# A trunk layer whose last matrix product is a seven-product block scheme: its stages in another order, other PSUM banks, tiles aligned to 512 bytes, scaled sums in place

## The chip, the cores and the metric

The kernel runs on one core of a Trainium2 chip, in one launch. Its time is the device time of that launch in microseconds (us). Three runs gave 753.96, 755.59 and 756.29 us; the median is 755.59 us. Engines are named as the profile names them: PE is TensorE (PEld its weight loads), DVE is VectorE, ACT is ScalarE, POOL is GpSimd, SP issues nearly all DMAs.

## The reference, cut to what matters

One decoder layer on x (512 tokens by 1024 channels, float32). The change touches the last part only, the dense MLP and what follows it:

```python
x = x + rms_norm(merged @ w_out[l], g_mix_post[l])
h = rms_norm(x, g_ff_pre[l])
ff = jnp.square(jax.nn.relu(h @ w_ff_in[l])) @ w_ff_out[l]     # 1024 -> 4096 -> 1024
x = x + rms_norm(ff, g_ff_post[l])
```

## The kernel before, in words

Every float32 operand of a matmul is split in a high part and a low part (`whi` and `wlo`, `ah` and `al`): ACT casts to get the high part, DVE subtracts to get the low part, and each product is three matmuls (`mm3`: high times high, high times low, low times high). All weights stream through one line of chunks of 512 KB in the order of the list `plan`: SP loads a chunk into one of three `raw` buffers, ACT and DVE split it into one of six pairs `whi`, `wlo`, and a raw buffer is loaded again as soon as DVE has made the low part from it. So a chunk that is six later waits until PE is done with the pair, and a load that is three later waits for DVE.

The MLP runs in four blocks b = 0 to 3 of 1024 hidden channels (`NB`, line 938 on). In each, eight tiles f of the first product (192 matmuls in all, called here the f1 stage, sums `accf` in two PSUM banks in turn) give the hidden activations; per tile ACT takes the relu out of PSUM (`rl`) and squares it (`ec`). Two tiles make a pair m: after the second, ACT and DVE make three split operands (`ah`, `al`, 128x768), DVE forms four sums of quarters (`ec`, 128x256), and ACT and DVE split those (`ah`, `al`, 128x1024). The second product is then done in 2x2 blocks with seven products instead of eight, in four stages over the four pairs: s1 (A11 and AQ, into banks `accx` and `accz`), s2 (A12, into `accy`), s3 (AN on into `accx`, A22 into a new `accy`), s4 (AR on into `accz`, AS on into `accx`). Between the stages `gather` adds a bank into the running sums `ys` in SBUF (ACT copies in block 0 where a sum is new, DVE adds otherwise). s1, s3 and s4 use sums of weight blocks that DVE makes in `block_sums` (`t`, `raw<-raw`), s2 plain ones.

Numbering of a block's chunks: 0 to 7 belong to f1 (0 and 1 to tiles 0 and 1, 2 and 3 to tiles 2 and 3, and so on), then come 8 to 11 for s1, 12 and 13 for s2, 14 to 17 for s3, 18 to 21 for s4.

Block 0 starts before the kernel's first PSUM pool is closed: its tiles 0 to 3 (`psf`) are done in halves of 256 columns in the banks of that pool, and the second PSUM pool opens after them. A PSUM pool hands out its banks in the order in which its names first appear. The first pool has `av` in bank 0, `tr` in 1 and 2, `z` in 3 and 4, `mm` in 5 to 7; `psf` 0 to 2 lie in 5 to 7, and `psf` 3 in bank 0. In the second pool before, `accf` has banks 0 and 1, `accx` 2 and 3, `accz` 4 and 5, `accy` 6 and 7. Until the second pool opens, ACT and DVE run in the order of the program (`act.on`, `dve.on`); from then on a scheduler in the compiler orders each engine's queue.

At the end, `scaled_out` takes the sum of squares of a finished sum on ACT (`junk`, with an accumulator) and multiplies it by the gain on DVE (`yg`); `finish_out` makes the root on POOL (`pr`), does the last scale and residual add on DVE, and stores. `junk` and `yg` share one ring of four buffers (`tmp`). The last tile's bank (`accz`, token tile 3) is filled in two halves of 256 columns, and the second half's matmuls wait for the first half's gather.

Of the kernel before, what the change touches and what calls it, by code (L numbers as in the profile page):

```python
# [9 lines left out]
F32 = mybir.dt.float32  # L10
# [4 lines left out]
ALU = mybir.AluOpType  # L15
PSUM = bass.MemoryType.PSUM

P = 128
T = 512
D = 1024  # L20
NT = T // P
# [27 lines left out]
def trunk_layer(ctx: ExitStack, tc: tile.TileContext, x, w_in, w_pool, pool_scale, gm_gain,  # L49
                w_spatial, b_spatial, w_br_sb, w_br_pool, w_br_gm, w_out, g_mix_pre,  # L50
                g_mix_post, g_ff_pre, g_ff_post, w_ff_in, w_ff_out, out):
    nc = tc.nc
    x2 = x[0]
    o2 = out[0]

    cst = ctx.enter_context(tc.tile_pool(name="cst", bufs=1))
    wp = ctx.enter_context(tc.tile_pool(name="wp", bufs=1))
    sm = ctx.enter_context(tc.tile_pool(name="sm", bufs=4))
    ht = ctx.enter_context(tc.tile_pool(name="ht", bufs=1))
    dram = ctx.enter_context(tc.tile_pool(name="dram", bufs=1, space=bass.MemoryType.DRAM))  # L60

# [7 lines left out]
    def slot(ring, name, dt=F32):  # L69
        return home[0].tile([P, T], dt, name=name, tag=ring, bufs=RINGS[ring])  # L70
# [81 lines left out]
    for b in range(NB):  # L152
        for f in range(0, FT, 2):
            use["f1", b, f] = plan_cols(ff_in_k, (b * FT + f) * P)


        for stage in ("s1", "s2", "s3", "s4"):
            use[stage, b] = range(len(plan), len(plan) + (2 if stage == "s2" else FT // 2))
            for m in range(0, FT // 2, 2 if stage == "s2" else 1):
                b11, b12, b21, b22 = (  # L160
                    ff_out_k[:, b * FT + 2 * m + o:b * FT + 2 * m + o + 1, c:c + 512]
                    for o in range(2) for c in (0, 512))
                if stage == "s2":
                    plan.append([ff_out_k[:, b * FT + 2 * m + 1:b * FT + 2 * m + 4:2, :512]])
                else:
                    plan.append({"s1": [b11, b12], "s3": [b22, b21], "s4": [b12, b22]}[stage])
                    derive[len(plan) - 1] = (stage, m)
# [95 lines left out]
    def cut(pair, s):  # L263
        return pair[0][:, s], pair[1][:, s]
# [97 lines left out]
    if True:  # L362
# [31 lines left out]
        two, rs, hns, pts = {}, {}, {}, {}  # L394
        for step in V_ORDER.split():
            what = step.rstrip("0123")
            t, g = ([int(c) for c in step[len(what):]] + [0, 0])[:2]
# [218 lines left out]
        pool = [None] * 2  # L616
# [259 lines left out]
    A11, A22, A12, AQ, AN, AS, AR = range(7)  # L876
# [25 lines left out]
    ys = [[None, None] for _ in range(NT)]  # L902
    yg = [[None, None] for _ in range(NT)]
    x1b = [None] * NT

    def product(ps, part, p, m, weights, new=True, c=WHOLE):

        left = tuple(x[:, part, p * P:(p + 1) * P] for x in parts[m])
        mm3(ps[:, c], left, cut(weights, c), new and m == 0, new and m == M - 1, not new)

    def block(which, p):
        return psum.tile([P, T], F32, name="acc" + which, tag=which, bufs=2)

    def gather(t, hf, ps, op, b, c=WHOLE):

        if ys[t][hf] is None:
            ys[t][hf] = ff.tile([P, T], F32, name="ys", tag="ys", bufs=8)
            act.activation(ys[t][hf], ps, AF.Copy, scale=1.0 if op == ALU.add else -1.0)
        else:
            dve.tensor_tensor(ys[t][hf][:, c], ys[t][hf][:, c], ps[:, c], op)  # L920

    def scaled_out(t, hf, c=WHOLE):
        n = hf + (c.start > 0)
        square_sum(ys[t][hf][:, c], twos[t][:, n:n + 1])
        if c.start == 0:
            yg[t][hf] = slot("tmp", "yg")
        dve.tensor_mul(yg[t][hf][:, c], ys[t][hf][:, c], gfpost[hf][:, c])

    def finish_out(t):
# [8 lines left out]
    M = FT // 2  # L938
    for b in range(NB):
        first = 0  # L940
        if b == 0:

            first = 4
            halves = slice(0, T // 2), slice(T // 2, T)
            wks = [Weights(("f1", b, f), ahead=2 - f) for f in (0, 2)]
            pss = [bank4("mm", f, "psf") for f in range(first)]
            for f in range(first):
                ff_in(pss[f], wks[f // 2], f % 2, halves[0])
                if f in (1, 2):
                    turn(f + 1)  # L950
            early.close()
            ff = ctx.enter_context(tc.tile_pool(name="ff", bufs=1, reuse_waits="tile"))
            home[0] = ff
            RINGS["tmp"] = 4
            gfpost = bcast_row(g_ff_post[0], [ff.tile([P, T], F32, name=f"gfpost{g}")
                                              for g in range(2)])
            for f in range(first):
                if f == 1:
                    Weights(("f1", b, first))[0]
                ff_in(pss[f], wks[f // 2], f % 2, halves[1])  # L960
                ff_act(f, pss[f])
            act.on = dve.on = False
            banks.close()
            psum = ctx.enter_context(tc.tile_pool(name="psum2", bufs=1, space=PSUM,
                                                  reuse_waits="tile"))
        for f in range(first, FT):
            if f % 2 == 0:
                wk = Weights(("f1", b, f))
            ps = block("f", f)
            ff_in(ps, wk, f % 2, slice(0, T))  # L970
            ff_act(f, ps)
        final = b == NB - 1
        if final:
            for i in range(2):
                pair = ff.tile([P, 2, D], F32, name="x1b", tag="ec", bufs=2)
                for t in (2 * i, 2 * i + 1):
                    x1b[t] = pair[:, t - 2 * i, :]
                    sp.dma_start(x1b[t], x1d[t])

        def stage(name, n, keep=False):  # L980

            wk = Weights((name, b), keep=keep)
            wk.tiles = [(i, j, k) for i in use[name, b] for j in range(len(plan[i]))
                        for k in range(plan[i][j].shape[1])]
            return lambda m, j: tile_of(wk, m * n + j)

        def tile_of(wk, i):
            i, j, k = wk.tiles[i]
            wk.ready(i)
            h, l = made[i][j]  # L990
            return h[:, k, :], l[:, k, :]

        two = range(2)
        x, z = ([block(w, p) for p in two] for w in "xz")
        w = stage("s1", 2)
        for m in range(M):
            for j, ps, part in (0, x, A11), (1, z, AQ):
                for p in two:
                    product(ps[p], part, p, m, w(m, j))
        for p in two:  # L1000
            gather(2 + p, 0, x[p], ALU.add, b)
            gather(p, 1, z[p], ALU.add, b)
        y = [block("y", p) for p in two]
        w = stage("s2", 1)
        for m in range(M):
            for p in two:
                product(y[p], A12, p, m, w(m, 0))
        for p in two:
            gather(2 + p, 0, y[p], ALU.add, b)
        if final:  # L1010
            for p in two:
                scaled_out(2 + p, 0)
        y = [block("y", p) for p in two]
        w = stage("s3", 2)
        for m in range(M):
            for j, ps, part in (0, x, AN), (1, y, A22):
                for p in two:
                    product(ps[p], part, p, m, w(m, j), j == 1)
        for p in two:
            gather(2 + p, 1, x[p], ALU.subtract, b)  # L1020
            gather(p, 0, y[p], ALU.add, b)
        w = stage("s4", 2, final)
        if not final:
            for m in range(M):
                for j, ps, part in (1, z, AR), (0, x, AS):
                    for p in two:
                        product(ps[p], part, p, m, w(m, j), False)
            for p in two:
                gather(2 + p, 1, z[p], ALU.add, b)
                gather(p, 1, x[p], ALU.subtract, b)  # L1030
                gather(p, 0, x[p], ALU.add, b)
            continue
        for m in range(M):
            product(z[0], AR, 0, m, w(m, 1), False)
        gather(2, 1, z[0], ALU.add, b)
        scaled_out(2, 1)
        for p in two:
            for m in range(M):
                product(x[p], AS, p, m, w(m, 0), False)
            gather(p, 1, x[p], ALU.subtract, b)  # L1040
            gather(p, 0, x[p], ALU.add, b)
            scaled_out(p, 1)
            scaled_out(p, 0)
            if p == 0:
                finish_out(2)
            finish_out(p)
        for c in HALVES:
            for m in range(M):
                product(z[1], AR, 1, m, w(m, 1), False, c)
            gather(3, 1, z[1], ALU.add, b, c)  # L1050
            scaled_out(3, 1, c)
        finish_out(3)
# [29 lines left out]
```

## Time and profile before

| what | value |
|---|---|
| median of three runs | 755.59 us |
| the profiled execution's own time | 756.68 us |
| its span, first to last instruction | 754.8 us |
| PE busy | 716.1 us (95%), 3320 matmuls |
| DVE, ACT, POOL busy | 494.7, 353.5, 53.8 us |
| HBM traffic | 89.2 MB, mean 118 GB/s over the span |

The profile is one execution. The span leaves out some 1.9 us of the run's own time. The MLP's blocks begin on PE at about 384 us (block 0, in halves), 481.0, 566.4 and 651.8 us; the last matmul ends at about 739.8 us. Times inside the span are counted from its start.

### The profile page before, as it was taken

To read this page: it belongs to the slowest core of one execution; us is meant where nothing else is said; L and a number is where in the kernel's file an instruction comes from. 1 tells how busy PE (TensorE), PEld (TensorE's weight loads), DVE (VectorE), ACT (ScalarE), POOL (GpSimd) and SP (SyncE) were. 2 spreads that over 40 slices of the span, in tenths; PEclk is the share of its full clock that TensorE was granted. 3 is DMA by queue.
4 is the path that set the end of the run, shared out by engine and by line. 5 is a ranking of instruction groups with operands and counts; after the bars stand their busy time and mean duration, and the time that the engine had idled before them with its cause. 6 is when DMAs were issued, how large, how long until landed. Compare 5 with 4: busy or idle time off the path is not lost.

```text
span 754.8 us, 9132 instructions
## 1 busy us (share of the span) xinstructions
PE 716.1 (95%) x3320; PEld 579.5 (77%) x3320; DVE 494.7 (66%) x755; ACT 353.5 (47%) x577; POOL 53.8 (7%) x103
## 2 busy tenths in 40 slices
PE   8999999999999999999993999999999999999891
PEld 5889887787878888888883777888788877888681
DVE  6646799786866443443756575566976678665974
ACT  6566756565453332233435465355334553355431
POOL 4001112212120000000310000000000000000000
PEclk9999999999999999999997899999999999999997
DMA  8363222312224333531345136532563335533612
GB/s 278 99 185 90 78 78 60 88 56 84 85 68 127 86 110 109 189 94 52 122 133 167 56 112 178 158 111 84 163 194 117 106 116 170 167 112 116 211 63 84
DMA packets 72431, 89.80 MB, mean 119 GB/s; under 512 B 4545, under 2 KB 49729, under 8 KB 72386
## 3 DMA queue, kind: packets, MB, share of 16 engines
q1 hardware_dynamic: 72384, 89.21, 37.9%
q8 instruction: 26, 0.43, 0.2%
q14 instruction: 19, 0.16, 0.1%
q10 hardware_dynamic: 2, 0.00, 0.0%
HBM read 85.01 MB, written 4.19 MB: 118 GB/s over the span
## 4 chain that ended last, share of the span: by engine, by line
PE 81%; DVE 8%; DMA 7%; ACT 2%; issue 1%; POOL 0%; SPq 0%; DVEq 0%; POOLq 0%; ACTq 0%
PE psc L82 26%; PE accf L82 19%; PE psb L82 6%; PE acc L82 5%; PE accy L82 5%; PE accx L82 5%; DMA raw<-in_w_ff_out_dram 4%; PE accz L82 3%; PE psv L82 3%; DVE wlo L82 2%; PE psgv L82 2%; PE z L82 1%; PE pt L82 1%; DVE raw L82 1%; PE av L82 1%
## 5 line engine op out<-in xcount | busy, mean ns | idle before, releaser
L82 DVE TENSOR_TENSOR wlo<-raw,whi 128x1024 fp32r<-128x1024 f32 (+1 forms) x145 | 166.7, 1154 | 124.5 <-ACT whi L82 124.0
L82 ACT CAST whi<-raw 128x1024 fp32r<-128x1024 f32 (+1 forms) x152 | 146.6, 972 | 163.6 <-PE accf L82 37.4
L82 PE MATMUL psc<-hT,whi 128*128 128x512 f32 x576 | 184.3, 401 | 0.0
L82 PE MATMUL accf<-hT,whi 128*128 128x512 f32 x448 | 142.4, 399 | 11.9 <-ACT rl L82 11.9
L82 PEld LDWEIGHTS psc<-hT,whi 128*128 128x128 f32 x576 | 104.0, 189 | 22.7 <-issue 1.5
L82 PE MATMUL psc<-hT,wlo 128*128 128x512 f32 x288 | 113.7, 395 | 0.0
L82 PEld LDWEIGHTS accf<-hT,whi 128*128 128x128 f32 x448 | 85.3, 191 | 32.5 <-ACT rl L82 12.1
L82 PE MATMUL accf<-hT,wlo 128*128 128x512 f32 x224 | 89.3, 399 | 0.0
L82 PEld LDWEIGHTS psc<-hT,wlo 128*128 128x128 f32 x288 | 54.2, 188 | 12.8
L82 PEld LDWEIGHTS accf<-hT,wlo 128*128 128x128 f32 x224 | 42.7, 191 | 10.3
L82 ACT CAST ah<-ec 128x768 fp32r<-128x768 f32 (+1 forms) x32 | 30.2, 943 | 32.6 <-DVE ec L82 32.1
L82 DVE TENSOR_TENSOR al<-ec,ah 128x768 fp32r<-128x768 f32 (+1 forms) x32 | 34.8, 1088 | 9.6 <-ACT ah L82 9.6
L275 POOL TENSOR_TENSOR pr<-pv,mhalf 128x1 f32<-128x1 f32 x8 | 4.8, 605 | 502.7 <-DVE pv L82 502.7
L82 PE MATMUL accx<-whi,al 128*128 128x512 f32 x96 | 37.9, 395 | 0.0
L82 PE MATMUL accx<-wlo,ah 128*128 128x512 f32 x96 | 37.9, 395 | 0.0
L82 PE MATMUL accx<-whi,ah 128*128 128x512 f32 x96 | 37.9, 395 | 0.0
L82 DVE TENSOR_TENSOR ec<-ec 128x256 f32<-128x256 f32 x64 | 26.7, 422 | 14.4 <-ACT ec L82 14.1
L82 DVE TENSOR_TENSOR_SCAN nb<-nb,zeros 128x128 f32<-128x128 f32 (+3 forms) x32 | 27.5, 864 | 7.5 <-POOL nb L473 7.0
L82 PE MATMUL accz<-whi,al 128*128 128x512 f32 (+1 forms) x68 | 26.3, 387 | 5.0 <-DVE al L82 5.0
L82 PE MATMUL accz<-whi,ah 128*128 128x512 f32 (+1 forms) x68 | 26.0, 383 | 1.3 <-DVE ys L82 1.3
L82 DVE TENSOR_TENSOR raw<-raw 128x512 f32<-128x512 f32 x32 | 22.0, 687 | 6.3 <-DMA raw<-in_w_ff_out_dram 6.3
L82 ACT CAST a<-pt 128x128 fp32r<-128x128 f32 (+3 forms) x32 | 13.6, 426 | 26.4 <-PE pt L82 26.4
(186 smaller groups left out, 1204.4 us busy)
## 6 DMA issues: line engine op xcount, KB each, us to landing
raw<-in_w_ff_out_dram SPq DMA_DIRECT2D x96, 256.0 KB, 3.0
raw<-in_w_in_dram SPq DMA_DIRECT2D x42, 512.0 KB, 3.9
raw<-in_w_ff_in_dram SPq DMA_DIRECT2D x32, 512.0 KB, 4.0
xt<-in_x_dram SPq DMA_DIRECT2D x16, 256.0 KB, 6.5
raw<-in_w_out_dram SPq DMA_DIRECT2D x8, 512.0 KB, 4.1
raw<-in_w_ff_out_dram SPq DMA_DIRECT2D x8, 512.0 KB, 3.6
raw<-in_w_br_sb_dram SPq DMA_DIRECT2D x4, 512.0 KB, 3.7
x1d<-xt SPq DMA_DIRECT2D x8, 256.0 KB, 2.9
```

Source lines behind the costliest of these rows:

```text
L82: i = op(*args, **kw).ins
L275: nc.gpsimd.tensor_tensor(r, v, mhalf, ALU.pow)
```

## The change

- The stages run s2, s1, s3, s4 instead of s1, s2, s3, s4, in the list of loads too: chunks 8 and 9 of a block are now s2's, 10 to 13 s1's.
- `accz` of block 0 is allocated as soon as the second PSUM pool opens, before the first `accf`, and `accy` before `accx`. So `accz` has banks 0 and 1, `accf` 2 and 3, `accy` 4 and 5, `accx` 6 and 7.
- During the four half-width tiles, the split ahead of tile 4 goes one chunk ahead and not three.
- In s3 each pair does `accy` first and then `accx`, but for the last pair. The gathers out of `accx` come before those out of `accz`.
- In the last block the scaled sums are written in place over `ys`, but for token tile 3.
- Three unused tiles of 384, 96 and 128 bytes a partition, each set to zero by POOL at the start, push the pools behind them. Before, `raw`, `whi`, `wlo` and all large tiles started 32 bytes past a multiple of 64; now they start on a multiple of 512.

```diff
--- before.py
+++ after.py
@@ -53,9 +53,17 @@
     x2 = x[0]
     o2 = out[0]
 
+
+    def spacer(name, n):
+        pool = ctx.enter_context(tc.tile_pool(name=name, bufs=1))
+        nc.gpsimd.memset(pool.tile([P, n], F32, name=name), 0.0)
+
+    spacer("space0", 96)
     cst = ctx.enter_context(tc.tile_pool(name="cst", bufs=1))
+    spacer("space1", 24)
     wp = ctx.enter_context(tc.tile_pool(name="wp", bufs=1))
     sm = ctx.enter_context(tc.tile_pool(name="sm", bufs=4))
+    spacer("space2", 32)
     ht = ctx.enter_context(tc.tile_pool(name="ht", bufs=1))
     dram = ctx.enter_context(tc.tile_pool(name="dram", bufs=1, space=bass.MemoryType.DRAM))
 
@@ -154,7 +162,7 @@
             use["f1", b, f] = plan_cols(ff_in_k, (b * FT + f) * P)
 
 
-        for stage in ("s1", "s2", "s3", "s4"):
+        for stage in ("s2", "s1", "s3", "s4"):
             use[stage, b] = range(len(plan), len(plan) + (2 if stage == "s2" else FT // 2))
             for m in range(0, FT // 2, 2 if stage == "s2" else 1):
                 b11, b12, b21, b22 = (
@@ -923,7 +931,7 @@
         n = hf + (c.start > 0)
         square_sum(ys[t][hf][:, c], twos[t][:, n:n + 1])
         if c.start == 0:
-            yg[t][hf] = slot("tmp", "yg")
+            yg[t][hf] = slot("tmp", "yg") if t == NT - 1 else ys[t][hf]
         dve.tensor_mul(yg[t][hf][:, c], ys[t][hf][:, c], gfpost[hf][:, c])
 
     def finish_out(t):
@@ -956,13 +964,14 @@
                                               for g in range(2)])
             for f in range(first):
                 if f == 1:
-                    Weights(("f1", b, first))[0]
+                    Weights(("f1", b, first), ahead=1)[0]
                 ff_in(pss[f], wks[f // 2], f % 2, halves[1])
                 ff_act(f, pss[f])
             act.on = dve.on = False
             banks.close()
             psum = ctx.enter_context(tc.tile_pool(name="psum2", bufs=1, space=PSUM,
                                                   reuse_waits="tile"))
+            z = [block("z", p) for p in range(2)]
         for f in range(first, FT):
             if f % 2 == 0:
                 wk = Weights(("f1", b, f))
@@ -991,7 +1000,16 @@
             return h[:, k, :], l[:, k, :]
 
         two = range(2)
-        x, z = ([block(w, p) for p in two] for w in "xz")
+        y = [block("y", p) for p in two]
+        w = stage("s2", 1)
+        for m in range(M):
+            for p in two:
+                product(y[p], A12, p, m, w(m, 0))
+        for p in two:
+            gather(2 + p, 0, y[p], ALU.add, b)
+        x = [block("x", p) for p in two]
+        if b:
+            z = [block("z", p) for p in two]
         w = stage("s1", 2)
         for m in range(M):
             for j, ps, part in (0, x, A11), (1, z, AQ):
@@ -999,25 +1017,21 @@
                     product(ps[p], part, p, m, w(m, j))
         for p in two:
             gather(2 + p, 0, x[p], ALU.add, b)
-            gather(p, 1, z[p], ALU.add, b)
-        y = [block("y", p) for p in two]
-        w = stage("s2", 1)
-        for m in range(M):
-            for p in two:
-                product(y[p], A12, p, m, w(m, 0))
-        for p in two:
-            gather(2 + p, 0, y[p], ALU.add, b)
         if final:
             for p in two:
                 scaled_out(2 + p, 0)
+        for p in two:
+            gather(p, 1, z[p], ALU.add, b)
         y = [block("y", p) for p in two]
         w = stage("s3", 2)
         for m in range(M):
-            for j, ps, part in (0, x, AN), (1, y, A22):
+
+            for j, ps, part in ((0, x, AN), (1, y, A22))[::1 if m == M - 1 else -1]:
                 for p in two:
                     product(ps[p], part, p, m, w(m, j), j == 1)
         for p in two:
             gather(2 + p, 1, x[p], ALU.subtract, b)
+        for p in two:
             gather(p, 0, y[p], ALU.add, b)
         w = stage("s4", 2, final)
         if not final:
```

In the rows below, from the built programs, each name carries its buffer's number. ACT, where block 0 goes from the half-width tiles (`psf`) to full-width ones (`accf`); `rl` of `psf` tile 1, 2 and 3 are here. Before:

```order
L82 CAST whi_3774<-raw_3758 128x1024
L82 ACTIVATE rl_3805<-psf_3591 128x512
L82 CAST whi_3900<-raw_3764 128x512
L82 ACTIVATE ec_3750<-rl_3805 128x512
L82 CAST whi_3966<-raw_3771 128x512
L82 CAST ah_3808<-ec_3750 128x768
L82 CAST whi_3900<-t1_3902 128x512
L82 CAST whi_3966<-t1_3968 128x512
L82 CAST ah_3808<-ec_3750 128x1024
L82 ACTIVATE rl_3843<-psf_3592 128x512
L82 ACTIVATE ec_3842<-rl_3843 128x512
L82 ACTIVATE rl_3870<-psf_3593 128x512
```

Now, beginning two rows further on in the program (`rl` and `ec` of tile 1 are the two rows ahead of the first), to the relu of the first full-width tile:

```order
L90 CAST ah_3808<-ec_3765 128x768
L90 CAST whi_3896<-raw_3773 128x1024
L90 CAST whi_3915<-raw_3779 128x1024
L90 CAST whi_3977<-raw_3894 128x1024
L90 CAST ah_3808<-ec_3765 128x1024
L90 ACTIVATE rl_3843<-psf_3607 128x512
L90 ACTIVATE ec_3842<-rl_3843 128x512
L90 ACTIVATE rl_3870<-psf_3608 128x512
L90 ACTIVATE ec_3842<-rl_3870 128x512
L90 CAST ah_3873<-ec_3842 128x768
L90 CAST ah_3873<-ec_3842 128x1024
L90 ACTIVATE rl_3935<-accf_3889 128x512
```

The relu and square of tile 1 have moved ahead of the cast of chunk 7 (`whi_3774` before, `whi_3896` now). Three whole casts, of chunks 7, 8 and 9, now stand between the two `ah` of pair 0. The relu of the first full-width tile stands behind `ah` 128x1024 of pair 1, as it did before (in rows not shown).

DVE in block 1, around the split of pair 3 (`al_4683` before, `al_4690` now). Before:

```order
L82 TENSOR_TENSOR raw_4723<-raw_4723,t1_4608 128x512
L82 TENSOR_TENSOR ec_4650<-ec_4650 128x256
L82 TENSOR_TENSOR raw_4723<-raw_4723 128x512
L82 TENSOR_TENSOR al_4683<-ec_4650,ah_4682 128x768
L82 TENSOR_TENSOR ec_4650<-ec_4650 128x256
L82 TENSOR_TENSOR wlo_4758<-raw_4704,whi_4757 128x1024
L82 TENSOR_TENSOR raw_4742<-raw_4742,t1_4630 128x512
L82 TENSOR_TENSOR ec_4650<-ec_4650 128x256
L82 TENSOR_TENSOR wlo_4785<-raw_4723,whi_4784 128x1024
L82 TENSOR_TENSOR raw_4742<-raw_4742 128x512
L82 TENSOR_TENSOR raw_4763<-raw_4763,t1_4698 128x512
L82 TENSOR_TENSOR al_4683<-ec_4650,ah_4682 128x1024
```

Now:

```order
L90 TENSOR_TENSOR wlo_4754<-raw_4642,whi_4753 128x512
L90 TENSOR_TENSOR raw_4732<-raw_4732,t1_4703 128x512
L90 TENSOR_TENSOR wlo_4754<-t1_4755,whi_4753 128x512
L90 TENSOR_TENSOR raw_4732<-raw_4732 128x512
L90 TENSOR_TENSOR ec_4657<-ec_4657 128x256
L90 TENSOR_TENSOR al_4690<-ec_4657,ah_4689 128x768
L90 TENSOR_TENSOR raw_4761<-raw_4761,t1_4726 128x512
L90 TENSOR_TENSOR ec_4657<-ec_4657 128x256
L90 TENSOR_TENSOR wlo_4777<-raw_4709,whi_4776 128x1024
L90 TENSOR_TENSOR ys_4109<-ys_4109,accy_4699 128x512
L90 TENSOR_TENSOR raw_4761<-raw_4761 128x512
L90 TENSOR_TENSOR ec_4657<-ec_4657 128x256
```

Ahead of `al` 128x768 there are now two half-width low parts of chunk 13 beside the two sums of chunk 15 (`raw_4723`, now `raw_4732`); the gathers out of `accy` have moved up between the sums of chunk 16.

DVE at the very end of the program, from the last scale of token tile 0. Before:

```order
L82 SCALAR_TENSOR_TENSOR yg_6229<-yg_6229,pr_6245,x1b_5956 128x512
L82 SCALAR_TENSOR_TENSOR yg_6225<-yg_6225,pr_6245,x1b_5956 128x512
L82 TENSOR_TENSOR ys_4277<-ys_4277,accz_5965 128x256
L82 TENSOR_TENSOR yg_6271<-ys_4279,gfpost0_3722 128x512
L82 TENSOR_SCALAR pv_6273<-two1_3169 128x1
L82 TENSOR_TENSOR yg_6298<-ys_4277,gfpost1_3723 128x256 x2
L82 SCALAR_TENSOR_TENSOR pv_6275<-two1_3169,pv_6273 128x1
L82 TENSOR_SCALAR pv_6316<-two3_3171 128x1
L82 SCALAR_TENSOR_TENSOR pv_6318<-two3_3171,pv_6316 128x1
L82 SCALAR_TENSOR_TENSOR yg_6271<-yg_6271,pr_6277,x1b_5956 128x512
L82 SCALAR_TENSOR_TENSOR yg_6267<-yg_6267,pr_6277,x1b_5956 128x512
L82 SCALAR_TENSOR_TENSOR pv_6320<-two3_3171,pv_6318 128x1
```

Now:

```order
L90 SCALAR_TENSOR_TENSOR ys_4292<-ys_4292,pr_6256,x1b_5963 128x512
L90 SCALAR_TENSOR_TENSOR ys_4203<-ys_4203,pr_6256,x1b_5963 128x512
L90 TENSOR_TENSOR ys_4290<-ys_4290,accz_6022 128x256
L90 SCALAR_TENSOR_TENSOR pv_6284<-two1_3184,pv_6282 128x1
L90 TENSOR_SCALAR pv_6325<-two3_3186 128x1
L90 TENSOR_TENSOR yg_6307<-ys_4290,gfpost1_3738 128x256
L90 SCALAR_TENSOR_TENSOR pv_6327<-two3_3186,pv_6325 128x1
L90 SCALAR_TENSOR_TENSOR pv_6329<-two3_3186,pv_6327 128x1
L90 SCALAR_TENSOR_TENSOR ys_4294<-ys_4294,pr_6286,x1b_5963 128x512
L90 SCALAR_TENSOR_TENSOR ys_4205<-ys_4205,pr_6286,x1b_5963 128x512
L90 SCALAR_TENSOR_TENSOR yg_6116<-yg_6116,pr_6331,x1b_5966 128x512
L90 SCALAR_TENSOR_TENSOR yg_6307<-yg_6307,pr_6331,x1b_5966 128x256 x2
```

The gain multiply of token tile 1 (`yg_6271`) no longer stands behind the last gather; the last gather (`ys_4290`, 128x256, before `ys_4277`) is now behind both last scales of tile 0, as before, and the order of the rest is the same.

## Rows read from the trace of the kernel before

**Rows 1.** The page, part 1: busy us, share of the span, instructions:

```profile
PE 716.1 (95%) x3320; PEld 579.5 (77%) x3320; DVE 494.7 (66%) x755; ACT 353.5 (47%) x577; POOL 53.8 (7%) x103
```

**Rows 2.** Waits of PE: total us, times, longest us:

```profile
PE accf L82 <- ACT rl L82: 11.9, 1, 11.9
PE accz L82 <- DVE al L82: 5.0, 4, 1.9
...
PE accz L82 <- DVE ys L82: 1.3, 1, 1.3
```

**Rows 3.** Timeline, block 0's start: start us, us, engine, instruction, [idle before <-releaser]:

```profile
402.32 1.05 ACT L82 CAST whi<-raw 128x1024 fp32r<-128x1024 f32 x1 [3.33 <-DMA raw<-in_w_ff_in_dram]
...
405.21 0.69 DVE L82 TENSOR_TENSOR t<-raw 128x512 f32<-128x512 f32 x1 [0.59 <-DMA raw<-in_w_ff_out_dram]
...
412.49 1.04 ACT L82 CAST ah<-ec 128x1024 fp32r<-128x1024 f32 x1 [4.23 <-DVE ec L82]
...
414.60 0.58 ACT L82 ACTIVATE rl<-psf 128x512 f32<-128x512 f32 x1
...
415.23 1.22 PE L82 MATMUL accf<-hT,whi 128*128 128x512 f32 x2 [11.88 <-ACT rl L82]
416.25 0.63 PE L82 MATMUL accf<-hT,wlo 128*128 128x512 f32 x1
...
420.09 0.58 PE L82 MATMUL accf<-hT,wlo 128*128 128x512 f32 x1
...
423.50 0.60 ACT L82 ACTIVATE rl<-accf 128x512 f32<-128x512 f32 x1 [3.26 <-PE accf L82]
```

**Rows 4.** Stretches: us, busy per engine, granted clock (share of full), DMA share, GB/s:

```profile
403.00:415.20 12.20, 0.35 (x3) 0.14 (x2) 9.66 (x15) 6.95 (x12) 0.00 (x0) 0.66 0.54 176
415.20:421.00 5.80, 5.77 (x15) 4.54 (x16) 3.12 (x6) 2.50 (x3) 0.00 (x0) 0.55 0.01 3
421.00:437.00 16.00, 16.00 (x70) 12.97 (x69) 8.43 (x14) 7.65 (x12) 0.00 (x0) 1.00 0.20 66
```

**Rows 5.** The chain that ended last, blocks 0 and 1:

```profile
481.01 41.60 PE accf L82 x179
...
566.43 41.78 PE accf L82 x179
```

**Rows 6.** Timeline, block 1, from the end of f1 on, DVE, ACT and PE:

```profile
525.42 1.05 ACT L82 CAST whi<-raw 128x1024 fp32r<-128x1024 f32 x1 [1.74 <-PE accf L82]
...
528.10 0.69 DVE L82 TENSOR_TENSOR raw<-raw,t 128x512 f32<-128x512 f32 x1 [0.37 <-DMA raw<-in_w_ff_out_dram]
...
529.65 0.95 DVE L82 TENSOR_TENSOR al<-ec,ah 128x768 fp32r<-128x768 f32 x1
...
536.98 0.50 PE L82 MATMUL accz<-whi,al 128*128 128x512 f32 x1 [1.13 <-DVE al L82]
```

**Rows 7.** Groups by shape: count, busy us, mean ns, idle before:

```profile
L82 DVE TENSOR_TENSOR wlo<-raw,whi 128x1024 fp32r<-128x1024 f32 x124 | 150.9, 1222 | 105.7 <-ACT whi L82 105.3
L82 DVE TENSOR_TENSOR ec<-ec 128x256 f32<-128x256 f32 x64 | 26.7, 422 | 14.4 <-ACT ec L82 14.1
L82 DVE TENSOR_TENSOR raw<-raw 128x512 f32<-128x512 f32 x32 | 22.0, 687 | 6.3 <-DMA raw<-in_w_ff_out_dram 6.3
```

**Rows 8.** The page, part 6: KB of an issue, median us to landing:

```profile
raw<-in_w_ff_out_dram SPq DMA_DIRECT2D x96, 256.0 KB, 3.0
```

**Rows 9.** Timeline, the end:

```profile
738.16 0.38 PE L82 MATMUL accz<-whi,ah 128*128 128x256 f32 x1 [1.30 <-DVE ys L82]
...
740.84 0.41 DVE L82 TENSOR_TENSOR ys<-ys,accz 128x256 f32<-128x256 f32 x1
742.44 0.63 ACT L82 ACTIVATE junk<-ys 128x512 f32<-128x512 f32 x1 [5.10 <-DMA out_dram<-yg]
...
748.34 0.42 ACT L82 ACTIVATE junk<-ys 128x256 f32<-128x256 f32 x1 [4.75 <-DMA out_dram<-yg]
...
750.08 1.54 DVE L82 SCALAR_TENSOR_TENSOR yg<-yg,pr,x1b 128x512 f32<-128x512 f32 x3 [1.03 <-POOL pr L275]
```

**Rows 10.** Timeline, the start, POOL:

```profile
0.80 0.52 POOL L331 MEMSET grow<- 128x512 f32 x1 [0.29 <-POOLq L1068]
```

## The prediction

> **What bounds the kernel now.** I read the page's busy shares first: PE is busy 95% of the span, no other engine over 66% [rows 1]. So the kernel's length is its matmuls plus the time PE stands still. The matmuls are the same 3320 after the change, so I looked for the standstills: PE's waits, then the timeline around each, then the stretches for the clock.
>
> PE's waits name one large one, 11.9 us for the relu `rl`, and 5.0 us in four waits for `al` [rows 2]. The timeline shows the large one at 403.3 to 415.2: the half-width tiles are done, and the first full-width matmul starts right as `rl` of `psf` tile 3 ends [rows 3]. Its weights were split long before. What it waits for is its bank: the first `accf` bank is bank 0, where `psf` 3 lies, read last of the four. ACT came to it late because its queue held a cast for which a load had to land (402.32) and an `ah` that waited 4.23 us for DVE [rows 3]. After the standstill the clock is at half: 0.55 granted over 415.2 to 421, full from 421 on [rows 4]; nine matmuls take 420.09 - 416.25 = 3.84 us, 0.427 each, against 41.60/179 = 0.232 in f1 [rows 3, 5]. The tile's 24 matmuls take until about 423.3 and not 415.2 + 24 x 0.232 = 420.8, so the half clock cost 2.5 us more (0.427 is the 1.2 GHz level, 512 columns a matmul).
>
> Each block also loses some time between f1 and the next f1. From 481.01, f1's 192 matmuls end at 525.5; the next f1 starts at 566.43 [rows 5]. The 168 matmuls between need 39.0 us, so about 1.9 us are lost, 1.3 of them in front of the `accz` matmul at 536.98, which waits for `al` of pair 3 [rows 6].
>
> The end: the last matmul ends at 739.8, the span at 754.8. In these 15 us ACT's last two `junk` wait 5.10 and 4.75 us for stores of `yg`, whose buffers they share [rows 9].
>
> **The change, part by part.** All sums are against the profiled execution, 756.68 us, 1.1 over the median of 755.59.
>
> *The banks.* `accf` now has banks 2 and 3, whose users (the transposes) are done by 391. The first full-width tile can start at 403.3: 11.9 + 2.5 = 14.4 us off. What is late next? Tile 6 needs bank 2 back, so `rl` of tile 4, which stands in ACT's queue behind `ah` 128x1024 of pair 1, which needs DVE's four `ec` of pair 1, which stand behind three `t` sums that need chunks 10 to 12. I walk that queue. Chunk 8 lands near 405.2, as the first `t` shows today [rows 3]; ACT casts chunks 8 and 9 to 407.3; DVE's low parts (1.22 each [rows 7], two `ec` between) end at 407.4 and 408.8 and free the buffers for chunks 11 and 12; a load lands 3.0 us after its issue [rows 8], some 3.5 for two halves; so the last `t` ends at 413.0, `al` at 413.9, four `ec` at 0.4 to 415.5, `ah` at 416.6, `rl` at 417.2. Tiles 4 and 5 end at 403.3 + 48 x 0.232 = 414.5. A new standstill of 2.7 us. Walking on the same way, f1 ends at 428.4; `al` 128x768 of pair 3 ends at 436.7, behind the two sums of chunk 15, which loads only once chunk 12 is split (430.5); s2 wants it at 428.4 + 20 x 0.232 + 0.3 = 433.3: 3.4 us. One gather out of `accx` is 0.7 late for s3. The next f1 then starts at 428.4 + 39.0 + 4.1 = 471.5, against 481.0: **9.5 us off**. The trace shows no such run of loads without PE standing still, so bounds: none of the new waits, 14.4 + 1.9 = 16.3; all of them a half longer (3.4) and a half clock after each of the two long ones (2.5 each), about 1.
>
> *s2 first, blocks 1 to 3.* s2 needs only the first `al` of a pair, but needs it sooner: for pair 3 at f1's end + 20 x 0.232 = +4.6 us, where s1 needed the second one at +10.2. With E = 525.5 in block 1 as the scale: ACT's casts of chunk 13 begin at E; DVE does one half low part, the first sum of chunk 15 (today at 528.10, waiting for its load [rows 6]; its buffer is now free 0.35 earlier), a second half, the second sum, an `ec`, then `al`: 527.7 + 0.6 + 0.6 + 0.6 + 0.35 + 0.9 = 530.75, E + 5.3. So 0.7 us of standstill, in place of 1.3; today the same `al` ends at 530.6 [rows 6]. The second `al` ends about E + 14 by the same walk and is wanted at E + 16. The wait between s2 and s3 for `accy` (0.3 a block) goes, as s1 now stands between; the gathers out of `accx` have only `accz`'s and `accy`'s matmuls, 12 x 0.232 = 2.8 us, to hide behind, and by DVE's queue the later one has 1 us to spare. 1.9 becomes 1.0 or so: **2.5 us off** over three blocks. Bounds: 5.7 (nothing left of it), -3 (1 us more each, as DVE is late by a load).
>
> *In place.* The `junk` no longer wait for stores. Then DVE decides: from the gather of the first half it has to do every scale itself, and the gain multiply now waits for `junk`, since it overwrites what `junk` reads. Walking DVE's queue from z's gather (729.88): the first half's gather ends at 738.5 (today 738.1, so PE's wait of 1.30 [rows 9] grows by 0.4); the second half's at 742.3, behind both scales of tile 0; `junk` at 742.9; the root at 743.95; the last three scales start at 744.7, against 750.08 [rows 9]: **5.4 us off**. Bounds: 6.9 if the last `junk` follows PE as closely as it can (741.5 against 748.34), 3 if each of the eight in-place multiplies adds its wait.
>
> *Alignment, three memsets.* The memsets stand ahead of `grow`'s, 0.52 us for 512 columns [rows 10], so some 0.3 us for 152 columns on POOL at the start, hidden behind the first weight load; bounds 0 and 0.4. The tiles' new starts: I take 0. DVE's 128x1024 takes 1222 ns and its 128x512 687 [rows 7], 1.04 ns an element, so nothing there looks like a penalty that could go. Loads may land some tenths sooner. The smaller look-ahead at tile 4 is in the walk.
>
> Sum: 9.5 + 2.5 + 5.4 = 17.4 off 756.68 is 739.3; from the median, 738.2. I say **739**.
>
> **Rivals.**
>
> *All the relief, none of the new waits.* 16.3 + 5.7 + 6.9 = 28.9: 727. For it: ACT and DVE are busy only 47% and 66% [rows 1]. Against: both queues are in order, and the places in the queue that I walked are written in the program.
>
> *Block 0 gives its gain back.* PE's standstill moves to tile 6 and to s2, both with a half clock behind them: block 0 gains 1, blocks 1 to 3 nothing, the end 5: 749. For it: 3.4 us is not far from what brought the clock down at 403. Against: a standstill of 1.3 us today costs no clock [rows 6].
>
> *Slower: s2 starved at every block.* `al` 128x768 of pair 3 stands behind two sums that wait for a load. If that load comes late in every block, PE stops in s2 four times. Gains elsewhere are 14.4 + 5.4 + 4 x 1.9 = 27.4, so this wins from 27.4/4 = 6.9 us a block, `al` at E + 11.5 with no half clock, or E + 9 with one. Today it ends at E + 5.1 [rows 6]. At 8.5 us a block the time is 762.
>
> *The matmul's pace.* At half clock a matmul takes 0.427, and half of that is 0.2135, but at full clock it takes 0.232 [rows 3, 5]. Something other than the clock takes 19 ns. If it is the start address of the operands, the aligned tiles save up to 3320 x 0.019, less for the short ones: about 55 us, 684. The Trainium skill ("TensorE: Matmul & The Clock Gate", section "Wait — 56ns, not 53.3ns?") gives 215.7 ns for 512 columns of bf16 at full clock, so it has this pace as possible; by it the sum would be some 50 us lower. Against: all large tiles of the trace start alike, so no row shows the other case, and the operands here are 4-byte.
>
> **How the numbers follow.** Forecast 739: 0.72. All relief, 727: 0.12. Given back, 749: 0.10. Starved, 762: 0.03. Pace, 684: 0.03. The forecast's own range is 732 to 746, from the block-0 bounds taken half-way; to leave out no more than 2 in 10, 730 to 747. Under 0.3% (2.3 us) nothing can be told from no change; the starved case is slower, 0.02 of the given-back one may end within it: faster 0.95, same 0.02, slower 0.03.
>
> **What would show it.** PE's wait for `rl` of 11.9 us gone and no half clock at 415; in its place a wait of some 3 us in front of the third full-width tile, and waits of `accy` for `al` in s2, longest in block 0; no `accz` for `al`; ACT's `junk` waiting for no store, and the last scale some 5 us nearer to the last matmul. The first f1 of block 1 at about 471, not 481. Matmul pace 0.232 as before. I am wrong if tile 4 still waits, if s2's waits exceed 5 us, or if the pace changes.

## The result, and the profile after

The changed kernel takes 726.88 us (median of 4 runs, 724.73 to 729.41) against 755.73 for the kernel before: ratio 0.9623, interval 0.9587 to 0.9660, so 28.5 us off the 755.6 shown ahead of the prediction. The forecast was 739 and its range 730 to 747: the sign is right, the time is 12 us below the forecast, and it lies below the range.

The profiled execution took 724.73 us. Its page, part 1 (busy us, share of the span, instructions), against [rows 1]:

```profile
PE 700.8 (97%) x3320; PEld 577.7 (80%) x3320; DVE 492.8 (68%) x755; ACT 353.2 (49%) x577; POOL 55.4 (8%) x106
```

Look at the busy time first. The 3320 matmuls are the same, yet PE is busy 15.3 us less (716.1 before). The standstills cannot show there, and the half clock behind the large one had cost 2.5 us, so no more than that can have gone with it. The rest must be the pace, the time from the start of one full-width matmul to the start of the next. The chain that ended last has it (start us, us, count). In the chain before, `accf` had 41.60 for 179 in [rows 5], 0.2324 each, and `psc`, a product in the front part of the layer:

```profile
235.42 11.16 PE psc L82 x48
```

Now:

```profile
233.19 10.88 PE psc L90 x48
...
464.19 40.59 PE accf L90 x179
...
531.24 2.72 PE accx L90 x12
```

40.59/179 = 0.2268, and 10.88/48 = 0.2267 against 11.16/48 = 0.2325: 5.7 ns less for each full-width matmul, in the front part of the layer too (`psc`), of which the diff touches nothing but the place of its tiles.

The waits of PE (total us, times, longest), against [rows 2]: the 11.9 for `rl` at tile 4 and the 5.0 of `accz` for `al` are gone; 3.0 for another `rl` and 3.1 of `accy` for `al` have come.

```profile
PE accy L90 <- DVE al L90: 3.1, 3, 1.2
PE accf L90 <- ACT rl L90: 3.0, 1, 3.0
...
PE accz L90 <- DVE ys L90: 1.3, 1, 1.3
```

Block 0, against [rows 3] (timeline; in brackets the idle time before and what ended it). The first full-width tile starts at 397.78, right behind the half-width ones. The standstill is at tile 6 now. It is for `rl` of tile 4, which stands behind an `ah` in ACT's queue, and that `ah` waits for DVE's `ec`:

```profile
410.30 1.04 ACT L90 CAST ah<-ec 128x1024 fp32r<-128x1024 f32 x1 [4.69 <-DVE ec L90]
411.25 0.59 ACT L90 ACTIVATE rl<-accf 128x512 f32<-128x512 f32 x1
...
411.89 0.94 PE L90 MATMUL accf<-hT,whi 128*128 128x512 f32 x2 [3.04 <-ACT rl L90]
...
413.06 1.05 PE L90 MATMUL accf<-hT,whi 128*128 128x512 f32 x2
413.91 0.63 PE L90 MATMUL accf<-hT,wlo 128*128 128x512 f32 x1
414.34 1.05 PE L90 MATMUL accf<-hT,whi 128*128 128x512 f32 x2
...
429.35 0.95 DVE L90 TENSOR_TENSOR al<-ec,ah 128x768 fp32r<-128x768 f32 x1
...
430.35 0.50 PE L90 MATMUL accy<-whi,al 128*128 128x512 f32 x1 [1.15 <-DVE al L90]
```

The stretches (us, busy per engine, granted clock, DMA share, GB/s) show a half clock behind that standstill as well, for 3.9 us:

```profile
397.70:411.80 14.10, 11.15 (x51) 8.91 (x49) 10.44 (x16) 7.74 (x10) 0.00 (x0) 1.00 0.44 141
411.80:415.70 3.90, 3.81 (x10) 2.99 (x11) 3.65 (x6) 3.84 (x8) 0.00 (x0) 0.56 0.22 70
```

The end, against [rows 9]: the last matmul ends at 713.76 + 0.28 = 714.04, the last `junk` waits for no store, and the last scales start 718.34 - 714.04 = 4.3 us behind the last matmul (750.08 - 739.8 = 10.3 before).

```profile
712.35 0.39 PE L90 MATMUL accz<-whi,ah 128*128 128x256 f32 x1 [1.34 <-DVE ys L90]
...
713.76 0.28 PE L90 MATMUL accz<-whi,al 128*128 128x256 f32 x1
...
716.18 0.42 ACT L90 ACTIVATE junk<-ys 128x256 f32<-128x256 f32 x1 [2.98 <-DVE pv L90]
...
718.34 1.53 DVE L90 SCALAR_TENSOR_TENSOR yg<-yg,pr,x1b 128x512 f32<-128x512 f32 x3
```

### The profile page after: what moved, and what is told of

It reads as the page before. It is cut to its first block, busy times and chain, and to the rows that moved or that the text cites. A ratio compares the mean times of both kernels' runs of the same rounds, so it can differ in the third digit from the quotient of the medians.

```text
span 723.0 us, 9131 instructions
## 1 busy us (share of the span) xinstructions
PE 700.8 (97%) x3320; PEld 577.7 (80%) x3320; DVE 492.8 (68%) x755; ACT 353.2 (49%) x577; POOL 55.4 (8%) x106
## 4 chain that ended last, share of the span: by engine, by line
PE 80%; DVE 8%; DMA 5%; ACT 3%; issue 2%; POOL 1%; SPq 0%; DVEq 0%; POOLq 0%; ACTq 0%
PE psc L90 25%; PE accf L90 16%; PE accx L90 9%; PE psb L90 6%; PE accz L90 6%; PE acc L90 6%; DMA raw<-in_w_ff_out_dram 4%; PE accy L90 4%; PE psv L90 3%; DVE wlo L90 2%; PE psgv L90 2%; PE z L90 1%; DVE ys L90 1%; ACT whi L90 1%; PE av L90 1%
## 5 line engine op out<-in xcount | busy, mean ns | idle before, releaser
L90 PE MATMUL psc<-hT,whi 128*128 128x512 f32 x576 | 182.2, 397 | 0.0
L90 PE MATMUL accf<-hT,whi 128*128 128x512 f32 x448 | 139.1, 392 | 3.0 <-ACT rl L90 3.0
L90 PE MATMUL accf<-hT,wlo 128*128 128x512 f32 x224 | 87.8, 392 | 0.0
L90 PE MATMUL accy<-whi,al 128*128 128x512 f32 x64 | 25.4, 396 | 3.2 <-DVE al L90 3.1
```

The source lines that it names most:

```text
L90: i = op(*args, **kw).ins
```

## Experiments

Theory after the result: the three unused tiles alone set the pace, because of where the operands start in SBUF; the other edits do what the prediction said. Rival: the pace comes with the other banks or the new order.

**Tile starts alone** (the kernel before and the three spacers):

```
...
+    spacer("space0", 96)
     cst = ctx.enter_context(tc.tile_pool(name="cst", bufs=1))
+    spacer("space1", 24)
     wp = ctx.enter_context(tc.tile_pool(name="wp", bufs=1))
...
+    spacer("space2", 32)
     ht = ctx.enter_context(tc.tile_pool(name="ht", bufs=1))
```

> The kernel before with the three unused tiles alone, so with its own stages, banks and tail. Theory (start address): a full-width matmul comes every 226.8 ns instead of 232.4, in every stage, and 2676 of the matmuls are full-width with a large tile streaming, so 15.0 us go: 740.7 us, with the 11.9 us wait for rl, the waits of accz for al and the late stores all still there. Rival (the pace comes with the other PSUM banks or the other order of the stages): the pace stays at 232 ns and the time at 755.6.

Measured: 745.28 us, ratio 0.9869 (0.9852 to 0.9887), 9.9 us off 755.6. Page part 1, the chain, and PE's waits:

```profile
PE 703.1 (95%) x3320; PEld 579.3 (78%) x3320; DVE 494.0 (67%) x755; ACT 353.2 (48%) x577; POOL 54.2 (7%) x106
```

```profile
249.43 10.88 PE psc L89 x48
...
473.22 40.59 PE accf L89 x179
```

```profile
PE accf L89 <- ACT rl L89: 11.1, 1, 11.1
PE accz L89 <- DVE al L89: 5.5, 4, 2.2
```

The pace is the new one and the old waits are all there: the rival falls. The size is below the expected 15.0. PE is busy 13.0 us less, and the two profiled executions differ by 12.3 (the one before lies 1.1 above its median, this one 0.9 below). Part of what is missing is in the front part of the layer. The stretches (us, busy per engine, granted clock, DMA share, GB/s) have it, two of the kernel before and the same two with the tile starts alone:

```profile
73.21:233.33 160.12, 159.73 (x782) 128.15 (x783) 129.79 (x233) 91.53 (x186) 31.84 (x66) 1.00 0.28 83
233.33:389.11 155.78, 154.38 (x716) 126.73 (x715) 75.75 (x106) 51.92 (x87) 9.06 (x11) 1.00 0.36 111
```

```profile
71.99:231.04 159.05, 158.43 (x782) 128.03 (x783) 129.79 (x233) 91.53 (x186) 31.95 (x66) 1.00 0.28 83
231.04:383.50 152.46, 151.03 (x716) 126.34 (x715) 75.42 (x106) 51.97 (x87) 9.07 (x11) 1.00 0.36 115
```

The second stretch is 3.3 us shorter, the first only 1.1, though over 500 of its 782 matmuls are full-width. In the first, small matmuls stand between them and DVE, ACT and POOL are busier; whether one of these holds the gain back was not tried.

**All but the tile starts** (the changed kernel without the three spacer lines):

> The changed kernel without the three unused tiles. Theory (start address): pace 232.4 ns everywhere again, stalls as in the changed kernel: 726.9 + 15.0 = 741.9 us, so the stage order, the banks and the in-place tail are worth 13.8 between them. Rival (the pace comes with banks or order): 727 and a pace of 227.

Measured: 737.57 us, ratio 0.9770 (0.9744 to 0.9797), 17.4 us off. The pace is the old one, and the standstills are those of the changed kernel; the chain, the timeline at tile 6 and at the `al` of pair 3, and PE's waits:

```profile
252.40 11.15 PE psc L87 x48
...
470.97 44.61 PE accf L87 x192
```

```profile
417.69 1.22 PE L87 MATMUL accf<-hT,whi 128*128 128x512 f32 x2 [2.77 <-ACT rl L87]
...
435.30 0.95 DVE L87 TENSOR_TENSOR al<-ec,ah 128x768 fp32r<-128x768 f32 x1
```

```profile
PE accy L87 <- DVE al L87: 2.2, 3, 1.2
```

So this kernel is what the prediction had worked out: 17.4 off expected, 17.4 measured. My expectation for it, 13.8, had given the pace too large a share. 17.4 and 9.9 make 27.3 of the 28.5; the rest is within the intervals.

**Which operand.** Two versions of the changed kernel, one with only `raw`, `whi`, `wlo` on multiples of 512 and one with only `hT` and all behind it, the others 32 bytes past. The first:

```
-    spacer("space2", 32)
+    spacer("space2", 40)
```

The second:

```
-    spacer("space1", 24)
+    spacer("space1", 32)
...
-    spacer("space2", 32)
+    spacer("space2", 24)
```

> The changed kernel with its third unused tile 32 bytes longer: raw, whi and wlo start on multiples of 512, but hT and all tiles behind it (ah, al, ys, the slots) 32 bytes past one. If the start of the streamed operand counts: 948 full-width matmuls stream whi or wlo and keep 226.8 ns (accx, accy, accz, acc, psv), those that stream hT (psc, accf) and the slots go back to 232.4, so 726.9 + 9.7 = 736.6. If the start of the stationary operand counts: psc and accf, whose stationary operand is whi or wlo, keep 226.8, and accx, accy, accz with ah and al as stationary go back, 726.9 + 6 = 733. If both must be aligned: all back, 742.

> The changed kernel with its second unused tile 32 bytes longer and the third 32 shorter: raw, whi and wlo start 32 bytes past a multiple of 512, hT and all tiles behind it on multiples of 512. If the streamed operand counts: psc and accf keep 226.8 ns, accx, accy, accz go to 232.4, 726.9 + 5.3 = 732.2. If the stationary operand counts: psc and accf go back, the second product keeps its pace, 726.9 + 9 = 736. If both: 742.

Measured: 739.06 us (ratio 0.9789, 0.9771 to 0.9806) and 737.81 (0.9786, 0.9753 to 0.9818): either way all of the pace's gain is lost (737.57 without the spacers). Of a matmul's two operands one is loaded by PEld and held still, the other is streamed. In the chains of the first version and then of the second, `psc` and `accf` stream `hT` against weights held still, and `accx` streams weights against `ah` and `al` held still:

```profile
252.75 11.20 PE psc L90 x48
...
471.13 44.78 PE accf L90 x192
...
539.72 2.80 PE accx L90 x12
```

```profile
253.54 11.20 PE psc L90 x48
...
473.65 44.80 PE accf L90 x192
...
542.42 2.80 PE accx L90 x12
```

0.2333 in every stage of both. So it is neither the streamed nor the held operand alone: one that starts 32 past is enough, on either side. That was the third of the outcomes expected.

**Which multiple.** The changed kernel with its first spacer 64 and 256 bytes longer (112 and 160 floats for 96).

> The changed kernel with its first unused tile 64 bytes longer, so that every large tile starts 64 bytes past a multiple of 512, the two operands of a matmul alike. If a start on a multiple of 64 is enough: 226.7 ns between full-width matmuls and 727 us as changed. If it takes a multiple of 128 or more: 232.4 to 233.3 and 738, as with starts 32 past.

> The same with the first unused tile 256 bytes longer: all large tiles start 256 past a multiple of 512. If 64, 128 or 256 are enough: 226.7 ns and 727 us. If only multiples of 512 will do: 233 ns and 738.

Measured: 725.12 and 727.80 us, one run each, and the fast pace in both; the chain of the first, then of the second:

```profile
464.50 40.59 PE accf L90 x179
```

```profile
465.85 43.52 PE accf L90 x192
```

A start on a multiple of 64 bytes is enough, 32 past it is not. Nor is it enough that the operands start alike: before, all of them started 32 past a multiple of 64. Other offsets were not tried. The Trainium skill ("SBUF — State Buffer", section "Specifications (TRN2)") gives SBUF lines of 16 bytes; by that a start 32 bytes past a multiple of 64, itself on a line's edge, would be as good as any. The two paces here do not follow lines of 16 bytes; the measurement decides.

**In place alone** (the kernel before and one line):

```
-            yg[t][hf] = slot("tmp", "yg")
+            yg[t][hf] = slot("tmp", "yg") if t == NT - 1 else ys[t][hf]
```

> The kernel before with only the scaled sums in place (but for token tile 3). Theory (the step of the prediction): no junk waits for a store, the last three scales start 5.4 us earlier against the last matmul; 755.2 - 5.4 = 749.8 us. Rival (DVE decides, each in-place multiply waits for its junk): 3 off, 752.

Measured: 749.63 us, ratio 0.9906 (0.9878 to 0.9934), 7.1 off (5.0 to 9.2). In the timeline the last matmul ends at 740.65 + 0.28 = 740.93 and the last scales start 4.3 us later, against 10.3: 6.0 of it can be seen there.

```profile
740.65 0.28 PE L82 MATMUL accz<-whi,al 128*128 128x256 f32 x1
...
743.08 0.42 ACT L82 ACTIVATE junk<-ys 128x256 f32<-128x256 f32 x1 [2.99 <-DVE pv L82]
...
745.22 1.54 DVE L82 SCALAR_TENSOR_TENSOR yg<-yg,pr,x1b 128x512 f32<-128x512 f32 x3
```

**Banks alone** (the kernel before with `accz` of block 0 taken first, and the shorter look-ahead):

```
-                    Weights(("f1", b, first))[0]
+                    Weights(("f1", b, first), ahead=1)[0]
...
+            z = [block("z", p) for p in range(2)]
...
-        x, z = ([block(w, p) for p in two] for w in "xz")
+        x = [block("x", p) for p in two]
+        if b:
+            z = [block("z", p) for p in two]
```

> The kernel before with only accz of block 0 taken as soon as the second PSUM pool opens (accz in banks 0 and 1, accf in 2 and 3) and the look-ahead of one chunk in front of tile 4; the stages in the old order. Theory: the 11.9 us wait and the half clock behind it go, a wait of about 3 us in front of tile 6 comes, and in the old order s1 meets al later than s2 would, so the net of block 0 is about 10.5: 755.2 - 10.5 = 744.7 us. Rival (given back: PE stands as long at tile 6 and at s1): 754.

Measured: 746.93 us, ratio 0.9875 (0.9842 to 0.9907), 9.4 off (7.0 to 11.9). The timeline at tile 4, the chain, and PE's waits:

```profile
405.37 0.63 PE L82 MATMUL accf<-hT,whi 128*128 128x512 f32 x2
```

```profile
472.44 41.60 PE accf L82 x179
```

```profile
PE accz L82 <- DVE al L82: 4.4, 4, 1.5
...
PE accf L82 <- ACT rl L82: 2.2, 1, 2.2
```

From the first `accf` matmul to the next f1 it is 472.44 - 405.37 = 67.1 us; before, from the end of the half-width tiles (403.3), 481.01 - 403.3 = 77.7. That is 10.6 us less, and 10.5 was expected.

**Order alone** (the changed kernel without spacers, bank change, look-ahead and in-place line):

> The kernel before with only the new order of the stages (s2, s1, s3, s4, in the list of loads too, accy before accx in s3, gathers out of accx before those out of accz); accf keeps banks 0 and 1, the tail and the tile starts are as before. Theory (the step of the prediction): 2.5 us off over blocks 1 to 3, and block 0 keeps its 11.9 us wait: 2.5 below the kernel before, with accy waiting for al 0.7 a block and accz not. Rival (the order alone starves s2): 3 us above it. A gain of 6 would say that the new order also takes the waits of block 0.

Measured: 754.11 us, ratio 0.9966 (0.9952 to 0.9980), 2.6 off. The waits of PE:

```profile
PE accf L87 <- ACT rl L87: 12.7, 1, 12.7
...
PE accy L87 <- DVE al L87: 1.1, 1, 1.1
PE accx L87 <- DVE ys L87: 0.6, 1, 0.6
```

The four waits of `accz` for `al` (5.0 in [rows 2]) are gone, less has come for them, and block 0 keeps its wait.

**Can more be had? No wait at tile 6** (the changed kernel; tiles 6 and 7 of block 0 in the idle `accx` banks):

```
-            ps = block("f", f)
+            ps = block("x" if b == 0 and f >= first + 2 else "f", f)
```

> The changed kernel with the tiles 6 and 7 of block 0 summed in the two accx banks (idle until s1) instead of the accf banks again, so that tile 6 need not wait for rl of tile 4. If that wait of 3.0 us and its half clock (8 matmuls at 0.427, 1.6 us) stand on the path that ends last: up to 4.6 off, 722. If the queues of ACT and DVE decide: al of pair 3 ends when it did, s2 waits for it as much longer, and nothing is gained: 727. I expect 2 us off, 725.

Measured: 728.34 us, ratio 0.9626 (0.9604 to 0.9649): the same as the changed kernel. The standstill has moved to s2, where PE now comes too early for `ah` and `al`:

```profile
427.04 0.50 PE L90 MATMUL accy<-whi,ah 128*128 128x512 f32 x1 [2.75 <-ACT ah L90]
430.45 0.80 PE L90 MATMUL accy<-whi,al 128*128 128x512 f32 x1 [2.68 <-DVE al L90]
```

`al` of pair 3 releases PE at 430.45, and in the changed kernel at 430.35. In block 0 the queues of ACT and DVE decide; my 2 us were not there.

**Part of s1 ahead of s2's last pair** (the changed kernel):

```
-        for m in range(M):
+        for m in range(M - 1):
             for p in two:
-                product(y[p], A12, p, m, w(m, 0))
+                product(y[p], A12, p, m, w2(m, 0))
...
         for m in range(M):
+            if m == 1:
+                for p in two:
+                    product(y[p], A12, p, M - 1, w2(M - 1, 0))
+                for p in two:
+                    gather(2 + p, 0, y[p], ALU.add, b)
             for j, ps, part in (0, x, A11), (1, z, AQ):
```

> The changed kernel with the first pair's share of s1 (12 matmuls, 2.7 us) moved in front of pair 3's share of s2, so that al of pair 3 is wanted 2.7 us later. If the four waits of s2 for al (gaps of 1.5, 0.5, 1.1 and 1.6 us between matmuls in the changed kernel, less the pitch of 0.23 each: 3.9) are simply lost time: 3.9 off, 723. If DVE is the later one anyway: the same time is lost at the second al of pair 3, in s1, and the time stays at 727.

Measured: 725.35 us, ratio 0.9582 (0.9558 to 0.9606). The wait of `accy` for `al` falls from 3.1 to 0.3, but `accx` now waits for gathers:

```profile
PE accx L90 <- DVE ys L90: 2.8, 3, 1.5
...
PE accy L90 <- DVE al L90: 0.3, 1, 0.3
```

By the medians this is 1.5 us better than the changed kernel, by the ratios 3.1, but the two intervals overlap, so a gain is likely and not shown. Of the versions that ran more than once it has the lowest median.

## Why the prediction was wrong, point by point

- **Alignment: the step that failed.** "The tiles' new starts: I take 0", since DVE's 1.04 ns an element showed no penalty. It measures 9.9 us (8.5 to 11.2), and it lies on PE, of which DVE's durations say nothing. The right place to look was named further down, among the rivals: at full clock a matmul takes 19 ns more than half of its half-clock time. But the rival had the size wrong as well (55 us, all of the 19 ns), and I gave it a chance of 0.03. 5.7 of the 19 ns belong to the start address. The nearest rows had left the term open between 0 and 55, so the range should have reached far below 730; I let the lack of a contrary row stand for evidence against. The range of 732 to 746 was not even what it was called: half of the way to block 0's bounds would be 735.6 to 743.2.
- **Banks.** Right in the path. Forecast 9.5 off, measured alone 9.4 (7.0 to 11.9; with the old stage order). The walk along ACT's and DVE's queues gave 2.7 for the standstill at tile 6 and `rl` ending at 417.2; without the spacers PE waits 2.77 and starts at 417.69. Two details were off: a half clock follows that standstill too (the clock of 0.56 over 3.9 us), and the longest wait for `al` is 1.2 and not 3.4. They nearly cancel, and not by luck alone: `al` of pair 3 comes when DVE's queue lets it (forecast to end at 436.7, ended at 436.25 without the spacers), so a PE slowed by the half clock waits less for it. The next f1 was forecast at 471.5 and starts at 470.97 there.
- **Order.** Right in sum, rougher in its parts. Forecast 2.5, measured 2.6 (1.5 to 3.6). Alone, blocks 1 and 2 have no wait of s2 for `al` that is worth a row, and block 3 has one of 1.1, where 0.7 a block was forecast; a gather out of `accx` is 0.6 late once, where 1 us was to spare. That the sum fits to a tenth is luck.
- **In place.** Right in kind, a little low. Forecast 5.4, in the traces 6.0, in the runs 7.1 (5.0 to 9.2). PE's last wait was to grow by 0.4 and did not (1.30 before, 1.34 in the changed kernel). The prediction's "last two `junk`" that wait for stores [rows 9] are the last and the last but two; the one between them waits for none.
- **Sum of these three.** Forecast 17.4, measured together 17.4 (15.3 to 19.3); the three alone add up to 19.1, with wider intervals.
- **Rivals.** "All the relief" gives 727 and would seem to have won, but by its number alone: its mechanism, no new waits, is not what the trace shows (3.0 for `rl` and 3.1 for `al`). "Given back" happened only where more was tried: with no wait at tile 6, what was gained there was lost in s2. "Starved" did not happen.

## What to carry to other kernels

Before an edit is priced at nothing because "only addresses change", compare the matmul's pace at full clock with half of its pace at half clock: what is left over is not the clock, and where a tile starts may be part of it. Here both operands, the streamed and the held one, had to start on a multiple of 64 bytes and not 32 past it; an unused tile in front of a pool was enough for that. And a wait at a bank is worth its own length less the time by which what comes next is late: walking the queues of the engines that make it gave 2.7 us where 2.77 came.

## What the runs showed of the hardware

- A full-width matmul on 4-byte operands takes 226.7 ns at full clock when both operands start on a multiple of 64 bytes, and 232.4 to 233.4 when either starts 32 past. At half clock the start makes no difference that shows: in the changed kernel, at a granted clock of 0.56, three matmuls take 414.34 - 413.06 = 1.28, 0.427 each, as in [rows 3]. The Trainium skill ("TensorE: Matmul & The Clock Gate", section "Wait — 56ns, not 53.3ns?") has 215.7 ns for 512 columns, in a part that measures bf16; no run here came below 226.7 on these operands, so where the other 13 ns over half of 0.427 go stays open.
- The durations on DVE and ACT show no difference by these starts (`wlo` 128x1024 takes 1222 ns before and 1221 with the tile starts alone, `whi` 1051 and 1053), nor does the landing of the 256 KB loads (3.0 us and 3.1). The 512 KB loads of `in_w_in` do, a little: by part 6 of the pages their median landing is 3.9 us in all six kernels whose `raw` starts 32 past, and 3.7 or 3.8 in all seven whose `raw` starts on a multiple of 64. What that is worth in time was not tried.
